# The first norm's modulation in four blocks of 256 columns instead of eight of 128

## The chip, the core and the metric

The kernel runs on one core of one Trainium2 chip. The metric is the device time of one execution in microseconds. Three runs of the kernel before took 1345.42, 1347.87 and 1349.15 us; the median, 1347.87 us, is the time before.

## The reference

One inference step of a network of two layers. 128 context tokens and 256 latent tokens, 384 columns in all, pass through each layer: a norm whose scale and shift come from a conditioning vector, three token mixers behind one joint input projection, an output projection, a second norm of the same kind and a feed-forward network. All is float32. What matters here is the start of the first layer:

```python
mod = (jax.nn.silu(cvec) @ p['w_mod'] + p['b_mod']).reshape(-1, 1, 6 * D_MODEL)
sh1, sc1, g1, sh2, sc2, g2 = jnp.split(mod, 6, axis=-1)
hn = _rmsnorm(x, p['g_norm1']) * (1 + sc1) + sh1
mix, new = _mixer(hn, p, ctx)          # begins with z = hn @ p['w_in']
x = x + g1 * mix
```

D_MODEL is 1024. The context tokens have one conditioning vector, the latent tokens another, so each of the six vectors of the modulation is made twice.

## The kernel before, in words

Activations lie with the 1024 features over 8 tiles of 128 partitions and the 384 tokens along the row (`x[n]`). A weight is loaded as float32 (`raw`), then split into a high part on ScalarE (`wh`, L150) and a low part, weight minus high part, on DVE (`wl`, L154); a product is three passes (high by high, high by low, low by high). The normed activations are split in the same way into `hh[n]` and `hl[n]`.

The program is a list of segments written out in order (`seg`, run by `run`). Each engine carries out its own instructions in the order in which this list emits them, and waits for others by semaphores. Before each segment `pump` (L121) issues the loads that have a free buffer, and emits the splits of loaded weights up to `split_lim`; a ring of four buffers holds raw weights (`RAWB`), at most three split weights are held at a time (`HB`). All weight loads go out on the queue of SP. Units of w_mod for the first norm use eight buffers of their own (m0 to m5, m10, m11).

The start, `head` and `plan_start` (L330 to L403), goes as follows. c is loaded, transposed and passed through silu (`sc`); x is loaded, its squares are summed on ScalarE, and TensorE transposes it. Then the shift and the scale of the first norm are made by blocks, n = 0 to 7, of 128 columns each: two loads of 512 KB (1024 rows of 128 columns, runs of 512 B), one for shift and one for scale; `mod` (L349) multiplies them with silu(c), four row groups of TensorE side by side; `copy` (L358) brings the sums from PSUM to SBUF by ScalarE; `post` transposes them (L372), adds up the four groups, adds the bias and the one (DVE, L376 to L380), and normalises tile n by `hn`. For an even tile `hn` is two operations of DVE (L650), two of ScalarE that write `hh` (L668), and two of DVE that write `hl` (L674). For an odd tile it is two of DVE (L650), three of ScalarE (L658, L664) and one of GpSimd that writes `hl` (L665). `row_fn` (L1198) then multiplies rows n*128 to n*128+127 of 512 columns of w_in with tile n: 12 products, summed over all n in four PSUM banks. The last row comes with the products of 32 gate columns (L1213). Behind it the dense products begin (L218), with the products of w_gate (L720) in the middle of the first.

The order of the segments sets how far these steps run ahead of each other. Per step s before: products of block s, copy of block s, `post` of block s-1, rows of tile s-2:

```python
        for s in range(KT + 2):
            if s < KT:
                for v in range(2):
                    self.seg([um[s][v]], lambda u, s=s, v=v: mod(u, s, v), 0)
            self.seg([], lambda s=s: copy(s), 0)
...
            if 1 <= s <= KT:
                self.seg([], lambda s=s: post(s - 1), 0)
...
            if s >= 2:
                self.seg([ur[s - 2]], lambda u, s=s: row_fn(u, s - 2))
```

`bcast` puts the tokens' reciprocal root mean squares on all partitions by a product with ones (L364); `x_rest` transposes the last two tiles of x (L321); `load_gl` loads the gates' columns on GpSimd's queue; `started_fn` is `begin`, which clears the buffer of w_gate on GpSimd (L1183) and loads it in eight pieces on SP (L1187).

## Time and profile before

| what | value |
|---|---|
| median of three runs | 1347.87 us |
| profiled execution, span from first to last instruction | 1348.4 us |
| mean granted clock of TensorE | 0.986 |
| TensorE busy | 1308.2 us, 97% of the span |
| DVE, ScalarE, GpSimd busy | 859.3, 596.5, 194.8 us |
| bytes moved | 198.51 MB, 147 GB/s over the span |

The profiled execution has no other time than its span; the median of the runs is 0.5 us less. A busy share says how long an engine had an instruction in work. The granted clock is the share of the full TensorE clock of 2.4 GHz; 0.5 is 1.2 GHz. The chain of waits is followed back from the last instruction, at each step to what released it. Line numbers are those of the kernel before; behind line 330 those of the changed kernel are larger by 5 to 7.

### The profile page before, as it was taken

The page shows a single profiled execution, that of the slowest core. Times are in us where ns is not written, and L with a number is a line of the kernel's source. Part 1 is how long each engine was busy: PE and PEld are TensorE (multiplying, and loading weights), DVE is VectorE, ACT ScalarE, POOL GpSimd, SP SyncE. Part 2 cuts the span into 40 slices and gives each one's busy share as a digit, 9 for nine tenths or more (in the row PEclk, how much of TensorE's full clock was granted, in tenths as well). Part 3 has the DMA queues.
Part 4 walks back from the last instruction along what each step waited for, and adds up shares of the span by engine and source line. Part 5 has one row for each costly group of instructions (what it writes and reads, how often), then busy time and mean ns, then how long its engine had stood idle before and what let it go on. Part 6 is the DMA issues. An engine that isn't in the chain of part 4 may idle for free.

```text
span 1348.4 us, 23432 instructions
## 1 busy us (share of the span) xinstructions
PE 1308.2 (97%) x9285; PEld 1215.7 (90%) x9285; DVE 859.3 (64%) x1501; ACT 596.5 (44%) x1104; POOL 194.8 (14%) x228
## 2 busy tenths in 40 slices
PE   6998999999999999999999899999999999999998
PEld 4787788889998999999988777888999999999998
DVE  4497876355468768675877987754546777544332
ACT  5655455343356333333446644543435643333221
POOL 1168000010033000000222850001101300000000
PEclk9898999999999999999999999999999999999999
DMA  9843454656543666665645325456344366444442
GB/s 287 229 97 94 129 143 137 166 144 171 158 129 103 193 175 188 187 191 166 201 133 152 102 82 163 121 154 172 96 125 126 93 186 189 141 125 120 122 137 61
DMA packets 297788, 198.51 MB, mean 147 GB/s; under 512 B 24560, under 2 KB 282384, under 8 KB 297680
## 3 DMA queue, kind: packets, MB, share of 16 engines
q1 hardware_dynamic: 296928, 196.68, 51.8%
q8 instruction: 73, 1.20, 0.4%
q0 software_dynamic: 608, 0.28, 0.1%
q14 instruction: 35, 0.29, 0.1%
q10 hardware_dynamic: 144, 0.07, 0.0%
HBM read 194.64 MB, written 2.36 MB: 146 GB/s over the span
## 4 chain that ended last, share of the span: by engine, by line
PE 81%; DVE 7%; DMA 3%; issue 3%; ACT 3%; POOL 1%; SPq 1%; ACTq 0%; DVEq 0%; POOLq 0%
PE d L218 59%; PE d L1411 8%; PE d L1343 2%; DMA m<-in_w_mod_dram 2%; PE m L471 2%; DVE wl L154 1%; DMA raw<-in_w_in_dram 1%; PE s L1103 1%; PE s L1058 1%; DVE m L791 1%; PE s L1092 1%; PE s L936 1%; DVE m L793 1%; DVE m L781 1%; SPq L1164 1%
## 5 line engine op out<-in xcount | busy, mean ns | idle before, releaser
L154 DVE TENSOR_TENSOR wl<-raw,wh 128x1024 fp32r<-128x1024 f32 (+2 forms) x274 | 330.1, 1207 | 129.1 <-ACT wh L150 123.5
L150 ACT ACTIVATE wh<-raw 128x1024 fp32r<-128x1024 f32 (+2 forms) x276 | 280.0, 1017 | 174.3 <-PE d L218 61.7
L218 PE MATMUL d<-hl,wh 128*128 128x384 f32 x1248 | 255.3, 342 | 0.0
L218 PE MATMUL d<-hh,wh 128*128 128x384 f32 x1248 | 251.5, 343 | 2.0 <-DVE vf L623 2.0
L218 PE MATMUL d<-hh,wl 128*128 128x384 f32 x1248 | 247.0, 340 | 0.0
L218 PEld LDWEIGHTS d<-hh,wh 128*128 128x128 f32 x1248 | 218.6, 188 | 17.3 <-issue 10.5
L218 PEld LDWEIGHTS d<-hh,wl 128*128 128x128 f32 x1248 | 223.5, 189 | 0.0
L218 PEld LDWEIGHTS d<-hl,wh 128*128 128x128 f32 x1248 | 221.0, 189 | 2.1 <-issue 0.6
L218 PE MATMUL d<-m,wh 128*128 128x384 f32 x896 | 165.9, 337 | 0.0
L218 PEld LDWEIGHTS d<-m,wh 128*128 128x128 f32 x896 | 155.7, 188 | 0.4 <-issue 0.4
L250 ACT ACTIVATE m<-tt 128x384 fp32r<-128x384 f32 x60 | 31.3, 525 | 160.2 <-DVE tt L1513 128.6
L218 PE MATMUL d<-m,wl 128*128 128x384 f32 x448 | 87.4, 336 | 0.0
L218 PEld LDWEIGHTS d<-m,wl 128*128 128x128 f32 x448 | 78.6, 188 | 0.0
L1411 PE MATMUL d<-m,wh 128*128 128x384 f32 x384 | 72.1, 340 | 0.0
L1411 PEld LDWEIGHTS d<-m,wh 128*128 128x128 f32 x384 | 65.9, 188 | 6.6 <-issue 6.6
L1431 POOL TENSOR_TENSOR m<-m,tt 128x384 f32<-128x384 f32 x16 | 16.9, 1074 | 341.9 <-DVE tt L1429 341.9
L560 POOL TENSOR_TENSOR ssq<-ssq,ev 128x384 f32<-128x384 f32 x18 | 29.4, 1636 | 251.3 <-ACT ev L558 251.2
L704 DVE SCALAR_TENSOR_TENSOR x<-d,modT,x 128x128 f32<-128x128 f32 x64 | 23.6, 413 | 54.3 <-PE d L218 46.5
L1513 DVE TENSOR_TENSOR tt<-tt,d 128x384 f32<-128x384 f32 x42 | 23.3, 554 | 51.6 <-PE d L218 51.6
L1394 ACT ACTIVATE tt<-d 128x384 f32<-128x384 f32 x48 | 23.6, 491 | 68.9 <-PE d L218 58.6
L1500 ACT ACTIVATE tt<-d 128x384 f32<-128x384 f32 x42 | 20.6, 489 | 70.0 <-PE d L218 66.4
L497 DVE SCALAR_TENSOR_TENSOR A<-raw,sc,A 128x1024 f32<-128x1024 f32 x35 | 47.1, 1344 | 0.0
(319 smaller groups left out, 1649.6 us busy)
## 6 DMA issues: line engine op xcount, KB each, us to landing
raw<-in_w_mod_dram SPq DMA_DIRECT2D x80, 512.0 KB, 3.9
raw<-in_w_in_dram SPq DMA_DIRECT2D x76, 512.0 KB, 4.0
raw<-in_w_ff_gate_dram SPq DMA_DIRECT2D x44, 512.0 KB, 4.8
raw<-in_w_ff_up_dram SPq DMA_DIRECT2D x44, 512.0 KB, 4.6
raw<-in_w_ff_down_dram SPq DMA_DIRECT2D x32, 448.0 KB, 4.6
m<-in_w_mod_dram SPq DMA_DIRECT2D x16, 512.0 KB, 7.3
raw<-in_w_in_dram SPq DMA_DIRECT2D x32, 256.0 KB, 3.9
raw<-in_w_out_dram SPq DMA_DIRECT2D x16, 512.0 KB, 4.1
```

The source lines that it names most:

```text
L150: nc.scalar.activation(h[:, f], w[:, f], AF.Copy)
L154: e.tensor_tensor(l[:, f], w[:, f], h[:, f].bitcast(F32), op=ALU.subtract)
L218: nc.tensor.matmul(ps, w[:, k * width + col:k * width + col + 128], xs[xi](k0 + k), start=first and n == 0, stop=last and n == tot - 1)
L250: self.nc.scalar.activation(h, v, AF.Copy)
L471: nc.tensor.matmul(st["ps"][32 * j:32 * j + 32], self.sc[:, kt, :], self.raw[u][:, j * 256:j * 256 + 256], start=kt == 0, stop=kt == KT - ...
L497: nc.vector.scalar_tensor_tensor(out=acc, in0=self.raw[u], scalar=s, in1=acc, op0=ALU.mult, op1=ALU.add)
L560: e.tensor_tensor(self.ssq, self.ssq, sq, op=ALU.add)
L704: nc.vector.scalar_tensor_tensor(out=self.x[n][:, c0:c1], in0=ps[:, c0:c1], scalar=self.modT[l][:, fg + n, v:v + 1], in1=self.x[n][:, c0:c ...
L1343: nc.tensor.matmul(vps[c], (self.hl if z else self.hh)[kk][:, c * 128:c * 128 + 128], w[:, k * 512:k * 512 + 512], start=kk == 0 and w is ...
L1394: nc.scalar.activation(tt, ps[:, 0:T], AF.Tanh, scale=0.5)
L1411: nc.tensor.matmul(ps[i], w[:, k * 256 + i * 128:k * 256 + i * 128 + 128], x2[xi](k), start=w is h and xi == 0 and k == 0, stop=w is lo an ...
L1513: nc.vector.tensor_tensor(tt, tt, pu, op=ALU.mult)
```

## The change

The modulation of the first norm is made in four blocks of 256 columns. A block has four loads of 512 KB in place of two: shift and scale, each in two halves of 512 rows, with runs of 1 KB. Count and bytes of the loads are the same. `mod` makes four products of 256 columns per load in place of eight of 128, `copy` moves 512 columns, `post` makes four transposes and the norms of two tiles. The four loads of a block stand together on SP, followed by two rows of w_in. The broadcast of the norm and the last transposes of x come before the first block's products, where they stood behind blocks 0 and 1. In step s now come: products of block s, copy of block s, row 2s-2, `post` of block s, row 2s-1. The two loads of c go out on ScalarE's queue in place of SP's. Comments are removed.

```diff
...
         ch = self.t("pr", [16, 128], bufs=4)
-        nc.sync.dma_start(ch[0:8], a["c_ctx"].rearrange("(k p) -> k p", p=128))
-        nc.sync.dma_start(ch[8:16], a["c"][0].rearrange("(k p) -> k p", p=128))
+        nc.scalar.dma_start(ch[0:8], a["c_ctx"].rearrange("(k p) -> k p", p=128))
+        nc.scalar.dma_start(ch[8:16], a["c"][0].rearrange("(k p) -> k p", p=128))
         self.ident = t("ident", [128, 128])
         nc.scalar.dma_start(self.ident, a["ident"])
...
             self.nc.scalar.activation(self.x[n], ps[:, 0:T], AF.Copy)
 
     def plan_start(self, rows, row_fn):
         nc, a = self.nc, self.a
+        NB = KT // 2
         st = {}
         w_mod = a["w_mod"][0]
-        um, ur = {}, {}
-        for n in range(KT + 1):
-            if n < KT:
-                um[n] = [self.unit(("mod0", n, v), self.w_cols(w_mod, v * D + n * 128), 0,
-                                   (0, 1, 2, 3, 4, 5, 10, 11)[(2 * n + v) % 8]) for v in range(2)]
-            if n:
-                ur[n - 1] = rows(n - 1)
-        def mod(u, n, v):
-            if v == 0:
-                st[n] = self.psa()
-            ps = st[n]
-            for k in range(KT):
-                j = k % 4
-                nc.tensor.matmul(ps[32 * j:32 * j + 32, v * 128:v * 128 + 128], self.sc[:, k, :],
-                                 self.raw[u][:, k * 128:k * 128 + 128], start=k < 4, stop=k >= 4,
+        um, ur, i = {}, {}, 0
+        for s in range(NB + 1):
+            if s < NB:
+                for v in range(2):
+                    for h in range(2):
+                        um[s, v, h] = self.unit(
+                            ("mod0", s, v, h),
+                            self.w_cols(w_mod, v * D + s * 256, nk=4, k0=4 * h, width=256), 0,
+                            (0, 1, 2, 3, 4, 5, 10, 11)[i % 8])
+                        i += 1
+            if s:
+                for n in (2 * s - 2, 2 * s - 1):
+                    ur[n] = rows(n)
+        def mod(u, s, v, h):
+            if v == 0 and h == 0:
+                st[s] = self.psa()
+            ps = st[s]
+            for j in range(4):
+                nc.tensor.matmul(ps[32 * j:32 * j + 32, v * 256:v * 256 + 256], self.sc[:, 4 * h + j, :],
+                                 self.raw[u][:, j * 256:j * 256 + 256], start=h == 0, stop=h == 1,
                                  tile_position=(0, 32 * j))
 
-        def copy(n):
-            self.split_lim = ur[n - 1] + 1 if 0 < n <= KT else 0 if n == 0 else 1 << 30
-            if n >= KT:
-                return
-            raw = self.t(("kn", "KA")[n % 2], [128, 256])
-            nc.scalar.activation(raw, st[n][:, 0:256], AF.Copy)
-            st[n] = raw
+        def copy(s):
+            self.split_lim = ur[2 * s - 1] + 1 if 0 < s < NB else 0 if s == 0 else 1 << 30
+            if s < NB:
+                raw = self.t("pT", [128, 512], bufs=2)
+                nc.scalar.activation(raw, st[s], AF.Copy)
+                st[s] = raw
 
         def bcast():
             self.prep_vec(0, 0)
...
             self.rs0 = self.t("ssq", [128, T])
             nc.vector.tensor_copy(self.rs0, ps[:, 0:T])
 
-        def post(n):
-            raw = st.pop(n)
+        def post(s):
+            raw = st.pop(s)
             pt = self.psa()
-            for v in range(2):
-                nc.tensor.transpose(pt[:, v * 128:v * 128 + 128], raw[:, v * 128:v * 128 + 128], self.ident)
-            m = self.modT[0]
-            ab = m[:, n:n + 9:8, :]
-            src = pt[:, 0:256].rearrange("p (v j c) -> p v c j", v=2, j=4)[:, :, 0:2, :]
-            nc.vector.tensor_reduce(ab, src, axis=AX.X, op=ALU.add)
-            vec = self.vec[0]
-            bm = vec[:, V_BMOD + n:V_BMOD + n + 9:8]
-            nc.vector.tensor_tensor(ab, ab, bm.unsqueeze(2).to_broadcast([128, 2, 2]), op=ALU.add)
-            nc.vector.tensor_scalar(m[:, 8 + n], m[:, 8 + n], 1.0, vec[:, V_N1 + n:V_N1 + n + 1],
-                                    op0=ALU.add, op1=ALU.mult)
-            self.hn(0, n, 8, 0, self.rs0)
+            for b in range(4):
+                nc.tensor.transpose(pt[:, b * 128:b * 128 + 128], raw[:, b * 128:b * 128 + 128], self.ident)
+            m, vec = self.modT[0], self.vec[0]
+            for h in range(2):
+                n = 2 * s + h
+                ab = m[:, n:n + 9:8, :]
+                src = pt.rearrange("p (v h j c) -> p h v c j", v=2, h=2, j=4)[:, h, :, 0:2, :]
+                nc.vector.tensor_reduce(ab, src, axis=AX.X, op=ALU.add)
+                bm = vec[:, V_BMOD + n:V_BMOD + n + 9:8]
+                nc.vector.tensor_tensor(ab, ab, bm.unsqueeze(2).to_broadcast([128, 2, 2]), op=ALU.add)
+                nc.vector.tensor_scalar(m[:, 8 + n], m[:, 8 + n], 1.0, vec[:, V_N1 + n:V_N1 + n + 1],
+                                        op0=ALU.add, op1=ALU.mult)
+                self.hn(0, n, 8, 0, self.rs0)
 
         self.modfin[0, 0] = self.modfin[0, 1] = iter(())
-        for s in range(KT + 2):
-            if s < KT:
+        self.seg([], bcast, 0)
+        self.seg([], self.x_rest, 0)
+        for s in range(NB + 1):
+            if s < NB:
                 for v in range(2):
-                    self.seg([um[s][v]], lambda u, s=s, v=v: mod(u, s, v), 0)
+                    for h in range(2):
+                        self.seg([um[s, v, h]], lambda u, s=s, v=v, h=h: mod(u, s, v, h), 0)
             self.seg([], lambda s=s: copy(s), 0)
-            if s == 0:
-                self.seg([], bcast, 0)
-            if 1 <= s <= KT:
-                self.seg([], lambda s=s: post(s - 1), 0)
-            if s == 1:
-                self.seg([], self.x_rest, 0)
-            if s == 4:
+            if s:
+                self.seg([ur[2 * s - 2]], lambda u, s=s: row_fn(u, 2 * s - 2))
+            if s < NB:
+                self.seg([], lambda s=s: post(s), 0)
+            if s == 2:
                 self.seg([], lambda: self.load_gl(0), 0)
-            if s == 4:
                 self.seg([], lambda: self.prep_vec(0, 1), 0)
-            if s == 6:
+            if s == 3:
                 self.seg([], self.started_fn, 0)
-            if s >= 2:
-                self.seg([ur[s - 2]], lambda u, s=s: row_fn(u, s - 2))
+            if s:
+                self.seg([ur[2 * s - 1]], lambda u, s=s: row_fn(u, 2 * s - 1))
 
     def setup(self):
         nc, a, t = self.nc, self.a, self.t
...
```

ScalarE at the start of the blocks, before: the copies (L358, into kn and KA), the splits of a row of w_in (L150, wh), and the norm's steps (ev and hh).

```order
L358 ACTIVATE kn_316<-s_87_295 128x256
L150 ACTIVATE wh_318<-raw_100 128x512
L658 ACTIVATE ev_327<-ev_327,modT_48_150 128x128
L658 ACTIVATE ev_327<-ev_327,modT_48_150 128x256
L664 ACTIVATE hh_33_135<-ev_327 128x384
L358 ACTIVATE KA_375<-s_101_354 128x256
L150 ACTIVATE wh_377<-raw_106 128x512
L668 ACTIVATE hh_34_136<-ev_386,modT_48_150 128x128
L668 ACTIVATE hh_34_136<-ev_386,modT_48_150 128x256
L358 ACTIVATE kn_425<-s_110_408 128x256
```

The same place now; the copy is L363 into pT, the norm's lines are larger by 6.

```order
L363 ACTIVATE pT_255<-s_72_226 128x512
L674 ACTIVATE hh_31_132<-ev_265,modT_47_148 128x128
L674 ACTIVATE hh_31_132<-ev_265,modT_47_148 128x256
L664 ACTIVATE ev_275<-ev_275,modT_47_148 128x128
L664 ACTIVATE ev_275<-ev_275,modT_47_148 128x256
L670 ACTIVATE hh_32_133<-ev_275 128x384
L363 ACTIVATE pT_307<-s_83_282 128x512
L150 ACTIVATE wh_309<-raw_102 128x512
L150 ACTIVATE wh_312<-raw_104 128x512
L674 ACTIVATE hh_33_134<-ev_346,modT_47_148 128x128
L674 ACTIVATE hh_33_134<-ev_346,modT_47_148 128x256
```

Before, copy and split of the next row stood ahead of the norm of one tile. Now the second copy and the splits of two rows stand behind the norms of both tiles of the first block.

ScalarE at the end of the blocks, before, from the copy of the last block to the split of the first dense weight (raw_501).

```order
L358 ACTIVATE KA_593<-s_135_576 128x256
L150 ACTIVATE wh_595<-raw_394 128x512
L668 ACTIVATE hh_38_140<-ev_604,modT_48_150 128x128
L668 ACTIVATE hh_38_140<-ev_604,modT_48_150 128x256
L150 ACTIVATE wh_626<-raw_444 128x512
L658 ACTIVATE ev_635<-ev_635,modT_48_150 128x128
L658 ACTIVATE ev_635<-ev_635,modT_48_150 128x256
L664 ACTIVATE hh_39_141<-ev_635 128x384
L150 ACTIVATE wh_657<-raw_501 128x1024
```

The same place now, from the copy of the last block to the split of the last row of w_in (raw_416).

```order
L363 ACTIVATE pT_479<-s_116_462 128x512
L150 ACTIVATE wh_481<-raw_334 128x512
L150 ACTIVATE wh_484<-raw_336 128x512
L674 ACTIVATE hh_37_138<-ev_513,modT_47_148 128x128
L674 ACTIVATE hh_37_138<-ev_513,modT_47_148 128x256
L664 ACTIVATE ev_523<-ev_523,modT_47_148 128x128
L664 ACTIVATE ev_523<-ev_523,modT_47_148 128x256
L670 ACTIVATE hh_38_139<-ev_523 128x384
L150 ACTIVATE wh_553<-raw_414 128x512
L150 ACTIVATE wh_556<-raw_416 128x512
```

Before, the split of row 6 stood ahead of the norm of tile 6, and that of row 7 ahead of the norm of tile 7; now both stand behind both norms.

SP at the first loads of w_mod (m) and of the rows of w_in (raw), before.

```order
L1164 DMA m_8_86<-in_w_mod_dram 128x8x128
L1164 DMA m_9_88<-in_w_mod_dram 128x8x128
L1164 DMA m_10_90<-in_w_mod_dram 128x8x128
L1164 DMA m_11_92<-in_w_mod_dram 128x8x128
L1177 DMA raw_94<-in_w_in_dram 128x512
L1164 DMA m_13_96<-in_w_mod_dram 128x8x128
L1164 DMA m_14_98<-in_w_mod_dram 128x8x128
L1177 DMA raw_100<-in_w_in_dram 128x512
L1164 DMA m_16_102<-in_w_mod_dram 128x8x128
L1164 DMA m_17_104<-in_w_mod_dram 128x8x128
```

The same place now.

```order
L1170 DMA m_8_86<-in_w_mod_dram 128x4x256
L1170 DMA m_9_88<-in_w_mod_dram 128x4x256
L1170 DMA m_10_90<-in_w_mod_dram 128x4x256
L1170 DMA m_11_92<-in_w_mod_dram 128x4x256
L1170 DMA m_12_94<-in_w_mod_dram 128x4x256
L1170 DMA m_13_96<-in_w_mod_dram 128x4x256
L1170 DMA m_14_98<-in_w_mod_dram 128x4x256
L1170 DMA m_15_100<-in_w_mod_dram 128x4x256
L1183 DMA raw_102<-in_w_in_dram 128x512
L1183 DMA raw_104<-in_w_in_dram 128x512
L1170 DMA m_73_231<-in_w_mod_dram 128x4x256
L1170 DMA m_74_237<-in_w_mod_dram 128x4x256
```

Two loads of w_mod and one row alternated from the second block on; now eight loads of w_mod come first, in runs of 256 columns, and then two rows at a time.

## Rows read from the trace of the kernel before

**Rows 1.** Busy time of each engine in stretches of 10 us. Columns: stretch, its length, then busy us and number of instructions of PE (TensorE), PEld, DVE, ACT (ScalarE) and POOL (GpSimd), granted clock, busy share of the DMA engines, GB/s.

```profile
10.00:20.00 10.00, 6.65 (x91) 3.81 (x91) 4.64 (x15) 4.25 (x11) 0.00 (x0) 0.83 1.17 302
20.00:30.00 10.00, 7.91 (x108) 6.35 (x108) 4.77 (x15) 4.14 (x9) 0.99 (x1) 1.00 1.16 305
40.00:50.00 10.00, 7.47 (x55) 6.40 (x54) 3.87 (x11) 4.18 (x9) 1.45 (x2) 0.67 0.76 205
50.00:60.00 10.00, 10.00 (x72) 7.70 (x72) 5.43 (x9) 6.73 (x11) 1.45 (x11) 0.99 0.58 138
70.00:80.00 10.00, 10.00 (x148) 9.71 (x147) 9.95 (x19) 2.69 (x5) 3.66 (x6) 1.00 0.26 58
```

**Rows 2.** The chain of waits, in order of time, in the first 90 us. Columns: start us, us, what.

```profile
16.77 8.37 DMA m<-in_w_mod_dram
...
34.95 9.17 DMA m<-in_w_mod_dram
44.16 1.08 PE s L349 x16
```

**Rows 3.** The timeline of the start, instructions of SP's queue, ScalarE, DVE and TensorE. Columns: start us, us, engine, line, operation, out and in, count, and in brackets the idle time before and what ended it.

```profile
0.74 0.41 SPq L258 DMA_DIRECT2D pr<-in_c_ctx_dram  x1
...
1.55 0.37 SPq L263 DMA_DIRECT2D m<-in_x_prompt_dram  x1
...
8.30 1.06 ACT L307 ACTIVATE m<-m 128x1024 f32<-128x1024 f32 x1 [0.24 <-DMA m<-in_x_sample_dram]
...
10.82 0.56 DVE L633 TENSOR_TENSOR sql<-ident,rs 128x384 f32<-128x384 f32 x1
...
13.18 1.65 PE L364 MATMUL s<-sql,one 128*128 128x384 f32 x2
14.76 1.84 PE L349 MATMUL s<-m,sc 128*32 128x128 f32 x32
16.53 0.44 PE L372 MATMUL s<-ident,kn 128*128 128x128 f32 x2
16.81 0.82 PE L321 MATMUL s<-ident,m 128*128 128x128 f32 x6
...
20.12 0.64 PE L349 MATMUL s<-m,sc 128*32 128x128 f32 x16 [1.02 <-DMA m<-in_w_mod_dram]
```

**Rows 4.** TensorE's timeline from the last two loads of the modulation to the first dense product.

```profile
42.66 0.65 PE L349 MATMUL s<-m,sc 128*32 128x128 f32 x16 [1.67 <-DMA m<-in_w_mod_dram]
44.16 1.08 PE L349 MATMUL s<-m,sc 128*32 128x128 f32 x16 [0.86 <-DMA m<-in_w_mod_dram]
...
45.52 0.67 PE L1224 MATMUL d<-hh,wh 128*128 128x384 f32 x1
...
49.79 0.65 PE L1224 MATMUL d<-hh,wh 128*128 128x384 f32 x1
...
52.27 0.85 PE L1213 MATMUL d<-hh,glw 128*32 128x384 f32 x8
...
54.99 0.44 PE L1224 MATMUL d<-hh,wh 128*128 128x384 f32 x1
...
57.19 1.57 PE L218 MATMUL d<-hh,wh 128*128 128x384 f32 x8
```

**Rows 5.** The norm of an even tile (from the reduction at 17.01) and of an odd one (from 21.17), on DVE, ScalarE and GpSimd.

```profile
17.01 0.17 DVE L376 TENSOR_REDUCE modT<-s 128x4 f32<-128x16 f32 x1 [1.59 <-PE s L372]
...
19.01 0.48 DVE L674 SCALAR_TENSOR_TENSOR hl<-ev,modT,hh 128x256 fp32r<-128x256 f32 x1 [0.15 <-ACT hh L668]
...
21.17 0.17 DVE L376 TENSOR_REDUCE modT<-s 128x4 f32<-128x16 f32 x1 [1.08 <-PE s L372]
...
23.17 0.52 ACT L664 ACTIVATE hh<-ev 128x384 fp32r<-128x384 f32 x1
...
23.85 0.99 POOL L665 TENSOR_TENSOR hl<-ev,hh 128x384 fp32r<-128x384 f32 x1 [17.54 <-ACT hh L664]
```

**Rows 6.** Copies and splits: ScalarE's copy of 256 columns, split of a row, DVE's low part of that row, ScalarE's copy of 384 columns.

```profile
16.68 0.38 ACT L358 ACTIVATE KA<-s 128x256 f32<-128x256 f32 x1 [3.28 <-PE s L349]
...
40.08 0.63 ACT L150 ACTIVATE wh<-raw 128x512 fp32r<-128x512 f32 x1 [1.09 <-DMA raw<-in_w_in_dram]
...
40.74 0.69 DVE L154 TENSOR_TENSOR wl<-raw,wh 128x512 fp32r<-128x512 f32 x1 [0.31 <-ACT wh L150]
...
55.16 0.49 ACT L1220 ACTIVATE vf<-d 128x384 f32<-128x384 f32 x1 [0.50 <-PE d L1213]
```

**Rows 7.** Stretches of 2 us, columns as in rows 1: the loads of x (runs of 4 KB) from 5 us, loads of w_mod from 11 us, the falls of the clock.

```profile
5.00:7.00 2.00, 1.60 (x7) 1.27 (x8) 0.00 (x0) 1.32 (x4) 1.14 (x9) 1.00 1.04 395
11.00:13.00 2.00, 0.90 (x25) 0.48 (x17) 0.37 (x1) 0.30 (x1) 0.00 (x0) 0.93 1.19 290
13.00:15.00 2.00, 2.00 (x11) 0.80 (x15) 0.35 (x2) 0.38 (x1) 0.00 (x0) 0.50 1.19 304
43.00:45.00 2.00, 1.14 (x28) 0.63 (x19) 0.00 (x0) 0.00 (x0) 0.50 (x2) 0.61 1.15 324
47.00:49.00 2.00, 2.00 (x8) 2.00 (x7) 1.76 (x4) 1.39 (x3) 0.00 (x0) 0.50 0.18 45
```

**Rows 8.** The clearing of w_gate's buffer on GpSimd and the eight loads of w_gate on SP.

```profile
42.98 0.52 POOL L1183 MEMSET m<- 128x512 f32 x1
...
43.53 6.18 SPq L1187 DMA_DIRECT2D m<-in_w_gate_dram  x8
```

## The prediction

> **What bounds the kernel now.** I read the windows of the ramp first. From 10 to 20 us the DMA engines move 302 GB/s with a busy share above 1, while TensorE works 6.65 of 10 us; from 40 to 50 us it works 7.47 of 10, at a mean granted clock of 0.67; from 50 us on it is busy 10.00 of 10 [rows 1]. So the change can only act before about 57 us, where the first dense product (L218) begins; what it shifts there is passed on whole, since TensorE has no gap behind it. The chain of waits comes second: between 16.77 and 44.16 us it lies on loads of w_mod (8.37 and 9.17 us in one piece), and the last of these releases the block's products at 44.16 [rows 2]. TensorE's timeline comes third: before 42.66 it is idle 1.67 us for that load and 0.86 us before 44.16, and the row that starts at 45.52 needs until 49.79, 4.27 us, where a row at the full clock (54.99 to 57.19) needs 2.20 [rows 4]. The ramp before is bounded by loading, with a clock loss at its end.
>
> **The change, part by part.** The product of block s with silu(c), its copy by ScalarE, four transposes, then the norm of two tiles (DVE and ScalarE) and two rows of w_in make one round; there are four rounds in place of eight. What decides is the order on ScalarE. Before, copy(s) and the split of the next row stand ahead of the norm of tile s-1, so a row's split never waits for the norm that is being made. Now the copy of block s+1 and the splits of rows 2s and 2s+1 stand behind the norms of both tiles of block s (the fences in the section on the change). That is a loop: transposes of block s, two norms in series, copy, split, row, transposes of block s+1.
>
> Its price, by rows. One even norm: from the reduction at 17.01 DVE goes on to its next work at 19.01 + 0.48 - 0.08 = 19.41, so 2.40 us. One odd norm: from 21.17 the last ScalarE step starts at 23.17 and ends at 23.69, 2.52 us [rows 5]. Adjoining ScalarE steps overlap by 0.1, so its copy can start 2.40 + 2.52 - 0.10 = 4.82 us behind the first reduction. The copy has 512 columns: 256 take 0.38 and 384 take 0.49 us, so I estimate 0.60, less the overlap 0.50; the split takes 0.63, and its low part on DVE is ready 0.69 + 0.03 later [rows 6]. First product of the row: 4.82 + 0.50 + 0.63 + 0.05 = 6.0 us behind the reduction. The row issues its products over 2.1 us, loses 0.4 to the wait for the low part of its weights (two products of 0.17 against 0.72), and four transposes follow (two take 0.44 [rows 3], four I put at 0.72): the next reduction comes 3.25 us behind the row's start. **The round takes 9.25 us.** TensorE's work in it is two rows (4.4), four units of the modulation at 0.64 [rows 3] and 0.72 of transposes, 7.7 us; loading it takes 2.1 MB of w_mod and 0.52 MB of w_in, 6.6 us at the 395 GB/s of the loads with 4 KB runs and 9.0 at the 290 GB/s measured where only 512 B runs are in flight [rows 7]. The loop is the longest of the three at either bound, so the wider runs (1 KB) earn little here.
>
> The start. The diagonal for the broadcast is ready at 10.82 + 0.56 = 11.38 [rows 3], and the modulation now stands behind broadcast and x_rest. Moving the two loads of c from SP to ScalarE's queue starts the loads of x 1.55 - 0.74 = 0.8 us earlier [rows 3], but x is waited for by three sums of squares on ScalarE, the last of which started at 8.30 when x had landed [rows 3]. The two issues (some 0.8 us) now stand ahead of ScalarE's table load, so the sums end no earlier, and I cost this part at nothing. Broadcast 1.65, x_rest 0.82 and four units (1.84 for 32 records at half clock, 0.64 per unit at full [rows 3]) end the first block between 11.4 + 0.85 + 0.8 + 2.6 = 15.6 (full clock) and 11.4 + 1.65 + 1.5 + 3.7 = 18.2 us (half clock). Rows 7 show the clock at 0.50 from 13 to 15 us after little work from 9.6 on, and the new order leaves TensorE idle there too; I take 17.0. The load is no later: 4 units behind x, 8.3 - 0.8 + 2.1 MB / 290 GB/s = 14.7.
>
> The sum. Copy and transposes: first reduction 18.5. Row 0 starts at 24.5, row 2 at 33.75, row 4 at 43.0; row 6 has no copy before it, only two splits, so it starts 8.75 later, at 51.75. Row 6 takes 2.5, the gates 54.99 - 52.27 = 2.72, row 7 2.20 [rows 4]: the first dense product starts at 59.2 in place of 57.19, **2.0 us later with the clock full throughout**.
>
> The clock is the second term. Row 5 ends at 43.0 + 3.15 + 2.2 = 48.35 and row 6 starts at 51.75: 3.4 us without any product. Before row 0 it is 2 to 3.5 us (block 1 is done between 21.0 and 22.5). In the trace of before, gaps of 1.67 and 0.86 us around 0.65 us of work were followed by a clock of 0.50 (0.61 over 43 to 45, 0.50 over 47 to 49 [rows 7]), and the row then took 4.27 in place of 2.20. Both new gaps are longer, so I expect a fall at each. The price of one fall lies between that of the first stretch (0.83 over 10 to 20 us is 3.4 us at half clock [rows 1], so 1.7 lost) and that at 44 us (the row lost 2.1, the product 1.08 - 0.64 = 0.4 [rows 3, 4], together 2.5). Two falls: 3.4 to 5.0, and nothing at the least if the clock holds; I take 4.4, in the upper part, since row 6, gates and row 7 follow without a break. The end of the ramp comes at 63.6, **6.4 us later**.
>
> Covered edits. The memset and the eight loads of w_gate now come behind the low part of tile 7 on GpSimd; before, they took 0.52 and 6.18 us on SP [rows 8]. At the full clock the last reduction is at 46.25, the norms and the low part end 6.1 later (2.40 + 24.84 - 21.17 [rows 5]), the memset at 52.9, the loads are issued by 56.3 to 59.1. Their product stands half a dense tile behind the end of row 7, at 61.3; a landing 2 us behind the issue just makes it, with more room at a lower clock. If that cover is gone, the loads of the next columns behind them on SP come later too, but they have two dense tiles of time. The gates' columns and the second half of the vectors ride between rows; nothing waits for them. The DMA count and the bytes stay.
>
> The Trainium skill, DMA: Bandwidth & Descriptors, section Specifications, holds that line rate is had from 512 B per transfer on. The trace does not agree: 290 GB/s with 512 B runs against 395 with 4 KB runs [rows 7]. By the rule the wider runs would give nothing, and the loading bound would stay near 9.0 us a round; by the rows it falls somewhere towards 6.6. Neither reaches the loop's 9.25, so the sum is the same.
>
> **Rivals.** (a) *Faster: loading stays the bound.* The point from which it decides is a loop shorter than a round's load, which the series of norms would have to undercut by 0.3 us at the slow rate. For it speaks that loading bounds the ramp now [rows 2]; against it, ScalarE's order. Price: w_mod's 8.4 MB at 290 to 395 GB/s and four rows of w_in behind x (7.5) land at 39.1 to 31.4; behind the last block come 0.65 of product, 1.7 of copy and split, rows 4 to 7 at 9.0, transposes 0.7, gates 2.7, so 14.8: the end at 46.2 to 53.9, 3 to 11 us earlier, about 1341 us. (b) *Same: the loop holds, but the clock does not fall, or the falls lie where TensorE waits anyway.* The gap of 1.02 us ahead of 20.12 [rows 3] was followed by no fall, the mean clock of 20 to 30 us is 1.00 [rows 1]; against it speaks that the two new gaps are two to three times as long. The end of the ramp at full clock is 0.6 (first block at 15.6) to 3.2 us late (at 18.2): 1348.5 to 1351. (c) *Slower still:* a third fall in the gaps of 1.4 us ahead of rows 2 and 4, 2 us more on top of the forecast: 1356 to 1359. (d) That a step of the norm overlaps the next more than the rows show would cut each round by up to 1 us; this lies inside (b).
>
> **How the numbers follow.** The profiled span is 1348.4 us and the median of the runs 1347.87, 0.5 less. Forecast: 1348.4 + 6.4 - 0.5 = 1354.3. Chances: forecast 0.58, (c) 0.08, (b) 0.25, (a) 0.09. Within 0.3% is within 4.0 us of 1347.87, which is about what a measurement of this kernel can tell from no change. Slower by more takes the forecast and (c): 0.66; the same takes (b) and the small end of (a): 0.26; faster takes the rest of (a): 0.08. The range holds the forecast with one to two falls, (b) and (c) without their tails, 1348.0 to 1359.0; the likeliest case alone has 1351.5 to 1357.
>
> **What would show it.** Right: ScalarE's copy of block 1 starts some 4.8 us behind the first reduction though the block's product is long done; rows 0, 2 and 4 start about 9.3 us apart; the chain of waits runs over DVE and ScalarE in the ramp and no longer over loads of w_mod; TensorE's idle time ahead of row 6 ends with a ScalarE split, near 3.4 us, and a granted clock of 0.5 follows; L218 begins at 61 to 66. Wrong: waits on loads of w_mod in the last two rounds, rounds shorter than 8.5 us, or a clock of 1.00 over rows 6 and 7, which alone would take the result back to no change.

## The result, and the profile after

The changed kernel takes 1359.58 us, median of four runs (1356.66 to 1361.22), against 1346.64 for the kernel before, now four runs (1343.86 to 1349.15): the ratio is 1.0097, 95% interval 1.0080 to 1.0114. It is slower, as forecast, but by 12.9 us where 6.4 were worked out, and 0.6 us above the end of the range.

The profiled execution of the changed kernel took 1361.18 us, with a span of 1359.4. First the stretches of 10 us, columns as in [rows 1]:

```profile
10.00:20.00 10.00, 6.45 (x44) 3.39 (x42) 2.87 (x11) 4.74 (x11) 0.00 (x0) 0.66 1.10 352
20.00:30.00 10.00, 5.13 (x51) 3.40 (x44) 4.67 (x14) 4.45 (x9) 0.99 (x1) 0.84 1.09 355
30.00:40.00 10.00, 8.30 (x59) 6.63 (x58) 4.51 (x14) 3.85 (x8) 1.01 (x1) 0.81 0.55 179
40.00:50.00 10.00, 8.53 (x61) 6.49 (x59) 4.51 (x18) 3.86 (x8) 1.63 (x2) 0.83 0.18 55
50.00:60.00 10.00, 6.61 (x28) 6.00 (x28) 4.51 (x15) 3.39 (x8) 1.21 (x3) 0.83 0.49 118
60.00:70.00 10.00, 9.50 (x61) 6.86 (x61) 3.53 (x4) 4.74 (x8) 0.91 (x12) 0.83 0.57 143
70.00:80.00 10.00, 10.00 (x52) 8.94 (x51) 3.60 (x5) 8.52 (x13) 0.00 (x0) 1.00 1.02 281
```

The loads now run at 352 to 355 GB/s until 30 us (302 to 305 before) and then fall to 179 and 55: they wait for the program. TensorE has gaps up to 60 us, and its granted clock is 0.81 to 0.84 in every stretch from 20 to 70, where before it was 1.00 from 20 to 30 and 0.99 from 50 on. The ramp is no longer bounded by loading.

Next the timeline from the start to the first dense product, columns as in [rows 3]; it answers to [rows 3] and [rows 4]:

```profile
0.74 0.40 SPq L263 DMA_DIRECT2D m<-in_x_prompt_dram  x1
...
1.67 0.38 ACTq L261 DMA_DIRECT2D ident<-in_ident_dram  x1
...
6.35 0.25 PE L294 MATMUL s<-ident,pr 16*128 16x16 f32 x1 [6.35 <-DMA ident<-in_ident_dram]
...
6.84 0.22 ACT L298 ACTIVATE rsmall<-cT 128x16 f32<-128x16 f32 x1 [3.48 <-DVE cT L296]
...
10.83 1.06 ACT L307 ACTIVATE m<-m 128x1024 f32<-128x1024 f32 x1
...
13.34 0.56 DVE L639 TENSOR_TENSOR sql<-ident,rs 128x384 f32<-128x384 f32 x1
...
14.05 1.62 PE L369 MATMUL s<-sql,one 128*128 128x384 f32 x2 [3.55 <-DVE vec L444]
15.46 1.49 PE L321 MATMUL s<-ident,m 128*128 128x128 f32 x6
16.88 3.48 PE L355 MATMUL s<-m,sc 128*32 128x256 f32 x32
...
21.77 0.17 DVE L383 TENSOR_REDUCE modT<-s 128x4 f32<-128x16 f32 x1 [5.51 <-PE s L377]
...
26.59 0.58 ACT L363 ACTIVATE pT<-s 128x512 f32<-128x512 f32 x1
...
27.74 0.69 PE L1230 MATMUL d<-hh,wh 128*128 128x384 f32 x1 [4.14 <-ACT wh L150]
...
38.89 0.44 PE L1230 MATMUL d<-hh,wh 128*128 128x384 f32 x1 [1.59 <-ACT wh L150]
...
49.35 0.44 PE L1230 MATMUL d<-hh,wh 128*128 128x384 f32 x1 [1.44 <-ACT wh L150]
...
59.51 0.45 PE L1230 MATMUL d<-hh,wh 128*128 128x384 f32 x1 [3.32 <-ACT wh L150]
...
69.00 1.57 PE L218 MATMUL d<-hh,wh 128*128 128x384 f32 x8
```

Rows 0, 2, 4 and 6 (27.74, 38.89, 49.35, 59.51) all wait for a ScalarE split, which stands behind the norm. No product waits for a load of w_mod. L218 begins at 69.00 in place of 57.19, 11.8 us later. From there to the end of the span it is 1290.4 us, before 1291.2: what the ramp loses is passed on whole in these two executions.

### The profile page after: what moved, and what is told of

Its sections match the earlier page's. It is cut to its first block, busy times and chain, and to the rows that moved or that the text cites. A ratio compares the mean times of both kernels' runs of the same rounds, so it can differ in the third digit from the quotient of the medians.

```text
span 1359.4 us, 23171 instructions
## 1 busy us (share of the span) xinstructions
PE 1311.4 (96%) x9157; PEld 1217.9 (90%) x9157; DVE 859.9 (63%) x1501; ACT 596.6 (44%) x1100; POOL 194.6 (14%) x228
## 4 chain that ended last, share of the span: by engine, by line
PE 80%; DVE 7%; ACT 3%; issue 3%; DMA 2%; POOL 1%; ACTq 0%; SPq 0%; DVEq 0%; POOLq 0%
PE d L218 59%; PE d L1417 8%; PE d L1349 2%; DMA raw<-in_w_in_dram 2%; PE m L477 2%; DVE wl L154 2%; PE s L1109 1%; PE s L1064 1%; DVE m L797 1%; PE s L1098 1%; PE s L942 1%; DVE m L799 1%; DVE m L787 1%; ACT wh L150 1%; DVE m L789 1%
## 5 line engine op out<-in xcount | busy, mean ns | idle before, releaser
L150 ACT ACTIVATE wh<-raw 128x1024 fp32r<-128x1024 f32 (+2 forms) x276 | 279.7, 1017 | 179.3 <-PE d L218 58.2
L218 PE MATMUL d<-hl,wh 128*128 128x384 f32 x1248 | 255.9, 343 | 0.0
L218 PE MATMUL d<-hh,wh 128*128 128x384 f32 x1248 | 251.7, 343 | 2.0 <-DVE vf L629 2.0
L218 PE MATMUL d<-hh,wl 128*128 128x384 f32 x1248 | 246.3, 339 | 0.0
L218 PEld LDWEIGHTS d<-hh,wh 128*128 128x128 f32 x1248 | 218.7, 188 | 17.0 <-issue 10.9
L218 PEld LDWEIGHTS d<-hl,wh 128*128 128x128 f32 x1248 | 221.4, 189 | 2.1 <-issue 0.3
L218 PEld LDWEIGHTS d<-hh,wl 128*128 128x128 f32 x1248 | 223.1, 189 | 0.0
L218 PE MATMUL d<-m,wh 128*128 128x384 f32 x896 | 165.9, 337 | 0.0
L218 PEld LDWEIGHTS d<-m,wh 128*128 128x128 f32 x896 | 155.7, 188 | 0.4 <-issue 0.4
L218 PE MATMUL d<-m,wl 128*128 128x384 f32 x448 | 87.4, 336 | 0.0
L218 PEld LDWEIGHTS d<-m,wl 128*128 128x128 f32 x448 | 78.6, 188 | 0.0
```

The source lines that it names most:

```text
L150: nc.scalar.activation(h[:, f], w[:, f], AF.Copy)
L218: nc.tensor.matmul(ps, w[:, k * width + col:k * width + col + 128], xs[xi](k0 + k), start=first and n == 0, stop=last and n == tot - 1)
```

## The experiments

Times below are medians, each with its ratio to the kernel before, run beside it on the same chip. As the stretch behind L218 took 1287.5 to 1293.0 us in the profiled executions, differences of 2 us are read from the start of L218 and not from the time. That start is itself of one execution, and it moves with the clock: the changed kernel and e2 have the same median and begin L218 at 69.00 and 66.49.

**e1, c's loads back on SyncE.**

```diff
-        nc.scalar.dma_start(ch[0:8], ...)
-        nc.scalar.dma_start(ch[8:16], ...)
+        nc.sync.dma_start(ch[0:8], ...)
+        nc.sync.dma_start(ch[8:16], ...)
```

> The changed kernel with one part undone: the two loads of c stand on SyncE's queue again, and ident is first on ScalarE's. Theory T1 (the set-up's loads are the first of three causes of the late start: ident, third on ScalarE's queue behind the two loads of c, landed at 6.35 us in the changed kernel's trace and not at 2.85, and held the first tanh, the norm's squares and the broadcast): ident lands near 2.9, the first block's products begin 2.0 to 3.3 us earlier, the products of line 218 start at 65.5 to 67.0 us and not at 69.0, and the time is 1356 to 1357.6 us. Rival R1 (the start is late by the wider blocks' loads, and the place of c's loads costs nothing, as the prediction had it): line 218 starts within 0.7 us of 69.0, time 1359 to 1360.

Measured: 1355.06 us (1.0082, 1.0056 to 1.0108). The first transpose of c starts at 2.82 us, the first reduction comes at 17.90, L218 at 63.63, 5.4 us earlier. TensorE's timeline, and the stretch around row 4:

```profile
11.60 1.62 PE L369 MATMUL s<-sql,one 128*128 128x384 f32 x2 [1.44 <-DVE vec L444]
...
14.43 2.06 PE L355 MATMUL s<-m,sc 128*32 128x256 f32 x32
...
45.35 0.44 PE L1230 MATMUL d<-hh,wh 128*128 128x384 f32 x1 [1.76 <-ACT wh L150]
```

```profile
40.00:50.00 10.00, 8.13 (x68) 6.53 (x68) 5.71 (x19) 4.21 (x9) 1.88 (x2) 1.00 0.33 77
```

The broadcast starts at 11.60 in place of 14.05: these 2.45 us are what the place of c's loads costs, and R1 falls. Two further parts of the 5.4 are clock. The first block's 32 products took 2.06 us in place of 3.48 (1.00 from 10 to 20 us), and from row 4 to row 6 it took 8.79 us in place of 10.16: the wait ahead of row 4, 1.76 us, was not followed by a fall. By the times alone the gain is not clear of noise, as the intervals of the ratios overlap (1.0056 to 1.0108, and 1.0080 to 1.0114).

**e2, ident ahead of c on ScalarE's queue.**

```diff
+        nc.scalar.dma_start(self.ident, a["ident"])
         nc.scalar.dma_start(ch[0:8], ...)
         nc.scalar.dma_start(ch[8:16], ...)
-        nc.scalar.dma_start(self.ident, a["ident"])
```

> The changed kernel with ident ahead of the two loads of c on ScalarE's queue; c's loads stay on that queue. T1 in the form that ident's place behind c is what costs: as in e1, ident near 2.9 us, line 218 at 65.5 to 67.0 us, 1356 to 1357.6 us. Rival R2 (it is c's own place on ScalarE's queue, whichever load stands third): the third load lands near 6 us again, now one half of c, the transposes of c start as late as 6.3 us, line 218 at 68.5 to 69.5 us and 1359 to 1360 us.

Measured: 1359.72 us (1.0108, 1.0086 to 1.0131), L218 at 66.49. Now it is c that TensorE waits for, until 7.00 us, and the broadcast starts at 14.70, no earlier than in the changed kernel. L218 alone lies where T1 put it, but that is clock: the 32 products took 1.93 us in place of 3.48, and from row 4 to row 6 it took 8.77 us, as in e1. Each fence below has ident's load among the DMA issues of the first 9 us (KB each, median us from issue to landing): the changed kernel, e1, e2.

```profile
ident<-in_ident_dram ACTq DMA_DIRECT2D x1, 64.0 KB, 4.5
```

```profile
ident<-in_ident_dram ACTq DMA_DIRECT2D x1, 64.0 KB, 1.9
```

```profile
ident<-in_ident_dram ACTq DMA_DIRECT2D x1, 64.0 KB, 3.8
```

In e1 and e2 ident is first on ScalarE's queue and issued at 0.74 us. It takes 1.9 us where x's first load goes out at 1.55, and 3.8 where that goes out at 0.74, beside it. So it is not the place behind c (my first form of T1 falls, R2 stands): moving c off SyncE let x's three loads of 512 KB go 0.8 us earlier, and the small loads that the start needs first then came in behind or beside them. That it is x's loads which delay them is read from these three traces; a run that holds back x's loads alone was not made.

**e3, broadcast and last transposes of x back in their old places.**

```diff
-        self.seg([], bcast, 0)
-        self.seg([], self.x_rest, 0)
...
             self.seg([], lambda s=s: copy(s), 0)
+            if s == 0:
+                self.seg([], bcast, 0)
...
                 self.seg([], lambda s=s: post(s), 0)
+            if s == 0:
+                self.seg([], self.x_rest, 0)
```

> The changed kernel with the norm's broadcast back behind the first block's products and the last transposes of x behind the first block's norm, where they stood before the change. T1 (the row of squares ends at 13.9 us, and the 32 products of the first block stand behind it and behind the transposes, 14.05 to 16.88): the first block's products begin at 14 to 15 us and its reduction comes 1.0 to 2.5 us earlier than 21.77; line 218 starts at 66.5 to 68.5 us, time 1357 to 1359. Rival (the first norm waits for the broadcast and the transposes anyway, so the order of the three on TensorE gives nothing): line 218 within 0.6 us of 69.0. Second rival (the first block then waits for its own loads and holds the broadcast behind it): line 218 later than 69.6.

Measured: 1354.91 us (1.0066, 1.0051 to 1.0081). The first reduction comes at 16.24, 5.5 us earlier, L218 at 63.19, some 3 us more than expected. The first block now waits for its own last two loads (12.54 and 14.05) and for nothing else, its clock is 1.00, and of the waits ahead of rows the one ahead of row 4 (1.77 us) brought no fall (8.78 us to row 6).

**e4, the rows one block later.**

```diff
-            self.split_lim = ur[2 * s - 1] + 1 if 0 < s < NB else 0 if s == 0 else 1 << 30
+            self.split_lim = ur[2 * s - 1] + 1 if 0 < s <= NB else 0 if s == 0 else 1 << 30
...
-        for s in range(NB + 1):
+        for s in range(NB + 2):
...
             self.seg([], lambda s=s: copy(s), 0)
+            if 1 <= s <= NB:
+                self.seg([], lambda s=s: post(s - 1), 0)
-            if s:
-                self.seg([ur[2 * s - 2]], lambda u, s=s: row_fn(u, 2 * s - 2))
-            if s < NB:
-                self.seg([], lambda s=s: post(s), 0)
+            if s >= 2:
+                self.seg([ur[2 * s - 4]], lambda u, s=s: row_fn(u, 2 * s - 4))
...
+                self.seg([ur[2 * s - 3]], lambda u, s=s: row_fn(u, 2 * s - 3))
```

> The changed kernel with the rows of w_in one block later: in each round the products of block s, its copy, the norm of block s-1 and then the rows of block s-2, so that the copy of a block stands ahead of the norm's splits on ScalarE's queue and two blocks are under way. T1 (the loop from a block's reduction over its norm's splits, the row's products and the next block's copy behind them sets the rounds of the changed kernel: 11.15, 10.46 and 10.16 us from one block's first row to the next, and in its gaps the granted clock falls to 0.81 to 0.84): the loop is broken, rounds come down to what the products take, 6 to 8 us, line 218 starts at 52 to 58 us, and the time is 1342 to 1348 us, no slower than before the change. Rival R3 (the wide block itself, its 32 products, its larger copy and its reduction, sets the round, or the loads do): rounds stay over 9.5 us and the time over 1355.

Measured: 1349.32 us (1.0023, 1.0008 to 1.0038), L218 at 57.52, within what T1 said; the time is 1.3 us above, and above the kernel before. The start is as late as in the changed kernel (first reduction 22.14), row 0 even later (29.16, behind block 2's products, which wait for loads until 27.37), but rows 2, 4 and 6 follow at 37.77, 42.40 and 46.67: the wait for ScalarE's splits is gone, and only row 6 still waits, 1.56 us, for the low part. Of the 11.8 us in the ramp this one edit gives back 11.5, and the falls of the clock in the loop's gaps are part of that.

**e5, the edits of e1 and e3 together.**

> The edits of e1 and e3 together: c's loads back on SyncE's queue, and the broadcast and the last transposes of x back behind the first block's products and its norm; only the blocks of 256 columns and the order of the rounds stay changed. Theory T1 (the two edits cure the same delay, and once it is gone the first block waits for its own loads, whose last product stood at 14.05 us in e3): the first reduction comes at 15.5 to 16.3 us, no more than 0.8 earlier than e3's 16.24, line 218 starts at 62.0 to 63.5 us, and the time is 1353 to 1355.5 us; what is left over before, 7 to 9 us, is the loop of the rounds and the clock. Rival (the two add up: 5.4 us by e1 and 5.8 us by e3): line 218 at 57 to 59 us and the time at that of the kernel before, 1346 to 1349.

Measured: 1356.21 us (1.0080, 1.0065 to 1.0096), L218 at 64.75 in an execution of 1359.55 us, the slowest of four. The two don't add up, and the rival falls, but T1's reduction, L218 and time were missed too, by 1.7, 1.3 and 0.7 us. The first reduction came at 17.99 and not by 16.3; the clock has a part in it: the units at 12.65 and 14.16 took 1.08 us each where 0.64 is the full clock. By the first reduction the start is worth 3.8 to 5.5 us (e1, e3, e5), once, by either edit.

**e6, idle products in TensorE's waits.** `n` is 14, 8, 8 and 20 ahead of rows 0, 2, 4 and 6.

```diff
             if s:
+                self.seg([], lambda s=s: fill(s, (0, 14, 8, 8, 20)[s]), 0)
                 self.seg([ur[2 * s - 2]], lambda u, s=s: row_fn(u, 2 * s - 2))
...
+        def fill(s, n):
+            ps = self.pd() if s == 1 else self.zfill
+            for _ in range(n):
+                nc.tensor.matmul(ps[:, 0:128], self.ident, self.ident)
...
+                self.zfill = st["z"][0]
```

> The changed kernel with idle work added that changes no output: 14, 8, 8 and 20 products of ident with itself, 128 columns each, stand on TensorE ahead of rows 0, 2, 4 and 6, where it waited 4.14, 1.59, 1.44 and 3.32 us in the changed kernel's trace. Theory T1c (the products of the rounds are late because the granted clock fell behind those waits, 0.81 to 0.84 in every stretch of 10 us from 20 to 70 us, which the prediction's two falls did not hold): the granted clock of 30 to 70 us is 0.93 or more, rounds come down from 11.15, 10.46 and 10.16 us to 9.0 to 9.6, line 218 starts at 62.5 to 66.5 us and the time is 1353 to 1357 us. Rival (the fall of the clock is not what the waits bring, or the added products themselves stand in the way of the rows): line 218 at 68.3 us or later, 1359 or more.

Measured: 1353.86 us (1.0064, 1.0050 to 1.0078), L218 at 62.77. The stretches of e6, columns as in [rows 1]:

```profile
20.00:30.00 10.00, 8.36 (x83) 6.50 (x76) 4.66 (x14) 4.45 (x9) 0.99 (x1) 1.00 1.08 355
...
40.00:50.00 10.00, 9.89 (x83) 8.33 (x84) 5.61 (x21) 3.85 (x8) 1.88 (x2) 1.00 0.27 69
50.00:60.00 10.00, 10.00 (x88) 8.42 (x90) 6.67 (x13) 5.38 (x9) 1.88 (x12) 1.00 0.29 73
```

And the first reduction of each block in e6, from DVE's timeline:

```profile
21.68 0.17 DVE L388 TENSOR_REDUCE modT<-s 128x4 f32<-128x16 f32 x1 [5.32 <-PE s L382]
...
30.86 0.17 DVE L388 TENSOR_REDUCE modT<-s 128x4 f32<-128x16 f32 x1 [1.95 <-PE s L382]
...
40.02 0.17 DVE L388 TENSOR_REDUCE modT<-s 128x4 f32<-128x16 f32 x1 [1.93 <-PE s L382]
...
49.26 0.17 DVE L388 TENSOR_REDUCE modT<-s 128x4 f32<-128x16 f32 x1 [1.93 <-PE s L382]
```

The granted clock is 1.00 (2.4 GHz) from 20 us on, and the rounds are 9.18, 9.16 and 9.24 us: the prediction's 9.25. TensorE did more and the ramp became 6.2 us shorter, so the waits cost the clock, and the clock cost 6.2 us in four rounds, or somewhat more: the 20 idle products ahead of row 6 run 4.62 us and end 0.7 us behind the split that the row needs. The time is 8.3 us over the kernel before, where the changed kernel's was 12.9.

**e7, a block's norm ahead of the rows of the block before.** The empty step keeps the low part of the rows' weights ahead of that norm on DVE.

```diff
+            self.seg([], lambda: None, 0)
+            if s < NB:
+                self.seg([], lambda s=s: post(s), 0)
             if s:
                 self.seg([ur[2 * s - 2]], lambda u, s=s: row_fn(u, 2 * s - 2))
-            if s < NB:
-                self.seg([], lambda s=s: post(s), 0)
```

> The changed kernel with one thing moved: the norm of a block (its transposes, reductions and scalings) stands ahead of both rows of the block before, not between them, with the rows' splits kept ahead of it on VectorE. Theory T1 (the round is a loop: a block's reduction, 6.0 us to its first row, 3.25 us through that row to the next block's transposes, since these stand behind the row): the next reduction comes 7.0 to 7.6 us after the one before in place of 11.15, 10.39 and 10.65 us, the first reduction stays at 21.8, line 218 starts at 57 to 61 us, and the time is 1348 to 1352 us. Rival (the wide blocks' products, or TensorE's own work of some 7 us a round at a fallen clock, set the round): reductions stay 9.5 us or more apart, line 218 at 65 us or later, 1355 or more.

Measured: 1353.67 us (1.0063, 1.0050 to 1.0077), L218 at 60.54. DVE's reductions in e7:

```profile
20.86 0.17 DVE L383 TENSOR_REDUCE modT<-s 128x4 f32<-128x16 f32 x1 [4.04 <-PE s L377]
...
28.01 0.17 DVE L383 TENSOR_REDUCE modT<-s 128x4 f32<-128x16 f32 x1
...
37.50 0.17 DVE L383 TENSOR_REDUCE modT<-s 128x4 f32<-128x16 f32 x1
...
45.79 0.17 DVE L383 TENSOR_REDUCE modT<-s 128x4 f32<-128x16 f32 x1
```

The first round takes 7.15 us, as expected, the next 9.49 and 8.29: in those the copy waits for its block's products, which stand behind both rows on TensorE (2.22 us of ScalarE's idle time before the copy at 35.14). So half of the expectation held: the loop is the order of the segments, and with that order mended the next link, products behind the rows, sets the round. L218 lies within T1's range, the time 1.7 us above it.

**e8, the edits of e1, e3 and e7.**

> The edits of e1, e3 and e7 together, with the blocks of 256 columns kept: c's loads on SyncE, the broadcast behind the first block's products, a block's norm ahead of the rows of the block before. Theory T1 (start by the loads, first reduction 15.5 to 16.3 us; second one when the loads of block 1 are in, near 22 us; then 7.0 to 7.6 us each): row 0 begins at 22 to 23.5 us, line 218 at 51 to 55 us, and the time is 1341 to 1345 us, below the kernel before. Rival (the loads of the later blocks or the clock take the gain back): line 218 at 57 us or later, 1347 or more.

Measured: 1348.34 us (1.0023, 1.0014 to 1.0032), L218 at 56.88, between what the two said. The gain is 12.1 us in the ramp, yet the kernel before isn't beaten, and by its time the rival holds: reductions at 18.00, 25.92, 35.07 and 43.34 show a first block in part at half clock (0.83 over 10 to 20 us) and the same two long rounds as in e7.

**e9, the move of c's loads alone, made in the kernel before.** The diff is e1's, the other way round.

> The kernel before the change with one part of the change alone: the two loads of c stand first on ScalarE's queue, ahead of ident, and x's loads go out first on SyncE's. Theory T1 (small loads issued beside x's large ones land 4 to 5 us after their issue, but in the kernel before this is covered: the broadcast stands at 13.18 us behind the first block's products, 1.8 us after its row of squares, and the later blocks wait for their loads until 44 us): ident and c land at 5.5 us or later, the first reduction comes 0.3 to 1.5 us later than 17.01, line 218 stays at 56 to 58.5 us, and the time is within 2 us of the kernel before. Rival (the late start passes on whole, as it does in the changed kernel, where undoing it gave 4.5 us): 1349 to 1352 us.

Measured: 1343.35 us against 1344.19 (0.9995, 0.9987 to 1.0004). From the timeline of e9:

```profile
7.02 0.26 PE L294 MATMUL s<-ident,pr 16*128 16x16 f32 x1 [7.02 <-DMA ident<-in_ident_dram]
...
14.73 0.89 PE L364 MATMUL s<-sql,one 128*128 128x384 f32 x2 [0.66 <-DVE vec L438]
...
17.03 0.17 DVE L376 TENSOR_REDUCE modT<-s 128x4 f32<-128x16 f32 x1 [0.82 <-PE s L372]
...
42.25 0.65 PE L349 MATMUL s<-m,sc 128*32 128x128 f32 x16 [1.02 <-DMA m<-in_w_mod_dram]
...
53.29 1.57 PE L218 MATMUL d<-hh,wh 128*128 128x384 f32 x8
```

The transposes of c come 4.2 us later than before, the broadcast 1.55 (14.73 against 13.18), and the first reduction at 17.03 in place of 17.01. That last step is luck of the clock: from broadcast to reduction it took 2.30 us at 1.00 over 10 to 20 us, and 3.83 before, at 0.83. In the order of the kernel before, the move is free in time: the first block's products stand ahead of the broadcast, and the later blocks wait for their loads until 42.25. In the changed order nothing covered it. The clock was 1.00 in all of e9's ramp, and L218 began 3.9 us before 57.19. Of these, 1.9 are the last load (42.25 against 44.16) and 2.0 the stretch behind it (11.04 us against 13.03): the profiled execution of the kernel before had a fall of the clock at 44 us that e9's had not.

**e10, loads and products of 256 columns in the order of the kernel before.** At even n stand the four units of a block and a copy of 512 columns, at odd n neither.

```diff
+        for n in range(KT + 2):
+            for s, v, h in plan.get(n, ()):
+                self.seg([um[s, v, h]], lambda u, s=s, v=v, h=h: mod(u, s, v, h), 0)
+            self.seg([], lambda n=n: copy(n), 0)
...
+            if 1 <= n <= KT:
+                self.seg([], lambda n=n: post(n - 1), 0)
...
+            if n >= 2:
+                self.seg([ur[n - 2]], lambda u, n=n: row_fn(u, n - 2))
```

> The changed kernel's loads and products in blocks of 256 columns, and for the rest the order of the kernel before: norms of 128 columns one by one, a block's copy ahead of the norm of the tile before it, row n-2 behind the norm of tile n-1, the broadcast behind the first block's products, c's loads on SyncE. Theory T1 (the wider loads are no harm, they moved 352 to 357 GB/s in place of 302 to 305; what made the changed kernel slower is the loop through the copy of the next block and the start): line 218 starts at 48 to 54 us, time 1338 to 1344 us, faster than the kernel before. Rival (a block of 256 columns is the harm itself: its loads come in pieces twice as large, so the first products and each pair's second half wait): line 218 at 56 us or later, 1346 or more.

**e11, as e10, with `post(n - 1)` ahead of the four units at even n.**

> As e10, with the norm of each odd tile ahead of the products of the next block of 256 columns on TensorE, so that it doesn't wait for their loads. Theory T1: the second norm begins 4 us or more before e10's and row 0 and row 1 run one behind the other; line 218 at 45 to 51 us, 1 to 4 us before e10's, time 1336 to 1341 us. Rival (the loads of the blocks or VectorE's norms, some 3 us a tile, set the pace in both): line 218 within 1 us of e10's.

Measured: e10 1343.95 us (0.9997, 0.9987 to 1.0007), L218 at 52.15; e11 1343.34 us (0.9993, 0.9981 to 1.0006), L218 at 51.31. The harm is not in the wide block (e10's rival falls), but there is no gain to measure either. e10 lies within T1's ranges, at the upper end of the time, and is not faster than the kernel before; for e11 the rival holds, with L218 0.8 us before e10's and the time 2.3 us above T1's. e11's timeline shows the last load that TensorE waits for:

```profile
38.14 0.64 PE L354 MATMUL s<-m,sc 128*32 128x256 f32 x8 [1.18 <-DMA m<-in_w_mod_dram]
...
51.31 1.57 PE L218 MATMUL d<-hh,wh 128*128 128x384 f32 x8
```

It is in 4.1 us before e9's last (42.25), but behind it stand four rows and the gates, 12.5 us, where in e9 three rows and the gates are left, 10.4 us. 2.0 us of the 4.1 remain (53.29 to 51.31).

**e12, the edits of e1 and e6 (11 idle products in place of 14).**

> The edits of e1 and e6 together: c's loads back on SyncE and idle products that change no output (11, 8, 8 and 20) ahead of rows 0, 2, 4 and 6. With the start as the prediction had it (its first reduction was at 18.5 us, e1's at 17.90) and the clock held, what is left is the prediction's loop alone, which put line 218 at 59.2 us at full clock. Theory T1: first reduction near 17.9, row 0 6.0 us behind it, 9.25 us from one block's first row to the next, line 218 at 58.3 to 60 us; time 1348.5 to 1351.5 us, so that loop, start and clock add up to the whole difference. Rival (start and clock overlap, the gain of one is part of the gain of the other): line 218 at 61 us or later, 1352 or more.

Measured: 1352.19 us (1.0047, 1.0031 to 1.0064), from e12's timeline:

```profile
17.72 0.17 DVE L388 TENSOR_REDUCE modT<-s 128x4 f32<-128x16 f32 x1 [4.97 <-PE s L382]
...
26.92 0.17 DVE L388 TENSOR_REDUCE modT<-s 128x4 f32<-128x16 f32 x1 [1.96 <-PE s L382]
...
36.09 0.17 DVE L388 TENSOR_REDUCE modT<-s 128x4 f32<-128x16 f32 x1 [1.94 <-PE s L382]
...
45.35 0.17 DVE L388 TENSOR_REDUCE modT<-s 128x4 f32<-128x16 f32 x1 [1.95 <-PE s L382]
...
58.86 1.57 PE L218 MATMUL d<-hh,wh 128*128 128x384 f32 x8
```

Rounds of 9.20, 9.17 and 9.26 us, L218 at 58.86 where the prediction's sum at full clock has 59.2. The time lies 0.7 us above what T1 said and would pass for the rival's; the stretch behind L218 took 1291.5 us in this execution, so the ramp, where the theories differ, decides for T1. Start and clock together are 10.1 us of the ramp. e1's 5.4 and e6's 6.2 come to more, but 1.5 of e1's are clock in its rounds; its first reduction comes 3.9 us earlier, and 3.9 and 6.2 make 10.1.

## Why the prediction missed

**Right: the loop and its price.** The copy of block 1 starts 4.82 us behind the first reduction (26.59 - 21.77; predicted 4.82), row 0 starts 5.97 behind it (6.0), and with the clock held the rounds are 9.2 us (9.25). The chain of waits, columns as in [rows 2], now reaches back only to DVE's low part of row 6's weights, and no load of w_mod is in it from there on:

```profile
59.49 1.09 DVE wl L154
...
60.62 0.44 PE d L1232
...
63.89 3.00 PE d L1219 x32
```

With that, and with no product waiting for w_mod before, rival (a) fell. The edits that the prediction called covered were: w_gate's loads went out at 60.52 and nothing waited for them.

**Wrong: "I cost this part at nothing", of the move of c's loads.** The first reduction came at 21.77, not 18.5: 3.3 us. The step asked when x lands and when the squares could then run, and took ident and c as given. ident landed 4.5 us after its issue beside x's loads, silu (6.84) and the squares came behind it, the last square at 10.83 in place of 8.30, and the diagonal was ready at 13.34 + 0.56 = 13.90 in place of 11.38. That is 2.5 of the 3.3. The rest is the clock of this execution, 0.66 over 10 to 20 us: from the diagonal to the end of the first block's products it took 6.5 us, where the bounds were 4.2 and 6.8 and 5.6 was taken. e9 shows how the error came about: in the kernel before, the move costs no time. The cover was the first block's products ahead of the broadcast, and the change itself removes it, so the two edits had to be costed together.

**Mis-sized: the clock, "two falls", 4.4 us.** From row 0 to row 6 it took 31.8 us in place of 27.25, and from row 6 to L218 9.5 in place of 7.4: 6.6 us, of which e6 gives back 6.2. The two falls that the sum held were about right: behind the waits ahead of rows 0 and 6 (4.14 and 3.32 us) the rounds took 1.9 and 2.0 us more than the sum's at full clock, against 2.2 each. What the sum lacked are the falls behind the waits ahead of rows 2 and 4, 1.59 and 1.44 us long, where it had 1.4 and no fall: 1.2 and 1.4 us. Rival (c) had one of the two. The row against it, the gap of 1.02 us ahead of 20.12 without a fall, was one case, and that gap is shorter than these. Nor does each such wait bring a fall: in e1, e2, e3 and e5 the wait ahead of row 4, 1.75 to 1.77 us, brought none. What decides it, no run here shows. So "two falls" were three or four.

Together 3.3 + 2.2 = 5.5 us more than the forecast. Of the 11.8 us between the two profiled executions, 10.1 are start and clock (69.00 - 58.86), not the loop: at full clock and with an early start it costs 58.86 - 57.19 = 1.7 us, some 0.5 of it e12's idle products ahead of row 6; 2.0 were forecast.

**A base that was itself late.** Every run listed here took 1.8 us more than its span, so the profiled execution before took some 1350.2 us and not 1348.4: 2.3 us above the median that the forecast started from, 3.6 above the median of four, and above the slowest run listed of that kernel (1349.23). Its ramp carried a fall of the clock and a late last load, and ended at 57.19, where those of e9, e10 and e11, as fast as the kernel before, ended at 53.29, 52.15 and 51.31. Against e9's ramp the loop alone costs 5.6 us and not 2.0. This fits the medians: e12, with start and clock mended, is 7.5 us over the kernel before, and e2's L218, 66.49, is 13.2 us behind e9's, where the changed kernel's median is 12.9 us above. The forecast added a difference against a slow execution to a median that lies lower. As one trace of the kernel before is kept, it is not shown that its ramp usually ends near 53 us.

Smaller slips. The row of 4.27 us at 45.52, from which the upper price of a fall was taken, holds two transposes at its end; by e9 the whole fall cost 2.0 us, not 2.5. In rival (a) 9.4 MB at 290 GB/s behind 7.5 us land at 40.0, not 39.1, which leaves it 2 us of gain at that end. And TensorE does have gaps behind the ramp (7.98 of 10 us busy from 80 to 90 us before); that a shift is passed on whole is shown by the two stretches behind L218, not by a lack of gaps.

## What to carry to other kernels

When an edit moves the first small loads of a kernel, look at what large loads go out beside them, and cost it in the order that the rest of the change leaves, not in the old one. Where one step of a pipeline is made coarser, follow each in-order queue for one round: a copy that gets behind the norm of the block before makes a loop, and the gaps of that loop can be paid a second time in the clock. One profiled execution can carry a fall of the clock that another has not; compare stretches at the same granted clock before pricing them, and set the profiled execution's own time against the median before adding a difference to it.
